# Eight small stores for the tail of one tile: moving bytes between DMA engines in a store-bound attention-score kernel

## The chip, the cores and the metric

One core of one Trainium2 chip. The time is device microseconds of one execution; every run told here is in the fast state, except the single run with labels, whose state is unknown. Before: median 204.15 us (204.05 to 204.17) in the first three runs.

## The reference

```python
batch, heads, seq, dim = 8, 8, 512, 64          # q, k: float32
def reference(q, k):
    scale = 1.0 / np.sqrt(q.shape[-1])
    return (np.einsum('bhqd,bhkd->bhqk', q, k) * scale).astype(np.float32)
```

16.8 MB are read and 67.1 MB written, so the stores are four fifths of the traffic.

## The kernel before

The output is made in 32 tiles of 2 MB, eight (`n`) in each of four units (`v`). A tile holds one pair of heads: head `h` on partitions 64h to 64h+63, and on each partition eight rows of 512 scores, 16 KB. Matmuls write two rows of scores (1024 columns) to PSUM, ScalarE and VectorE take turns in scaling them into the tile `o`, and one DMA of 128 rows of 16 KB stores it. Four buffers of `o` rotate.

```python
P = 128; RO = 8; U = S // RO                      # U = 64
out_r = out.rearrange("(v b) (n h) (u i) k -> v (b n) (h u) (i k)", b=2, h=2, i=RO)
out_pool = ctx.enter_context(tc.tile_pool(name="out", bufs=4))
...
def evacuate(dst, src):                           # alternates ScalarE, VectorE
    ...
def scores(v, n):
    kT, qz = ts[v]
    o = out_pool.tile([P, RO, S], f32, name="o")
    for i in range(0, RO, 2):
        ps = psum_pool.tile([P, 2, S], f32, name="ps")
        for w in range(2):
            pinned(nc.tensor.matmul(out=ps[:, w, :], lhsT=qz[:, i + w, n, :],
                                    rhs=kT[:, n].rearrange("d m s j -> d (m s j)"),
                                    start=True, stop=True))
        evacuate(o[:, i:i + 2, :], ps)
        yield
    src = o.rearrange("p i k -> p (i k)")
    nc.sync.dma_start(out=out_r[v, n], in_=src)
```

`qz` holds q of both heads, block-diagonal with zeros, so one matmul over 128 rows makes both heads' scores. Loads, casts and transposes run ahead of this and are not touched.

## Time and profile before

| | before |
|---|---|
| time, us | 204.15 |
| span in the profile, us | 202.3 |
| packets of the data queue q1 | 5760 |
| one 16 KB packet, start to start, us | 0.607 |
| last packet of the last DMA engine, us from the span's start | 201.01 |
| mean of the 16 engines' last packets, us | 198.53 |

The profile lines are in the prediction below. How to read them: in the slices each digit is the busy share of a fortieth of the span; DMA at 9 from end to end with every compute engine lower says that the data movement is the bound. In the groups, the figures before the bar are count and form, after it busy time and mean, and last the idle time before and what ended it. In the table of windows the columns are the window, its length, five engines' busy time, the granted TensorE clock, the mean busy share of the 16 DMA engines and GB/s.

The page says nothing about single DMA engines. The trace has a record of each packet with its start, duration, size and queue, without the engine. In it a packet as a rule starts 3 to 4 ns before another one ends, which is taken for the one ahead of it on its engine, and each transfer of 128 rows gives eight packets and a completion of 4 bytes to each chain; linked so, all records fall into sixteen rows, as many as the page counts DMA engines. "Row" below means such a chain, and where an engine is spoken of, it is such a row. It is worked out from the trace, not printed by it; where two rows end a packet in the same nanoseconds, they could be exchanged.

### The profile page before, as it was taken

The page shows a single profiled execution, that of the slowest core. Times are in us where ns is not written, and L with a number is a line of the kernel's source. Part 1 is how long each engine was busy: PE and PEld are TensorE (multiplying, and loading weights), DVE is VectorE, ACT ScalarE, POOL GpSimd, SP SyncE. Part 2 cuts the span into 40 slices and gives each one's busy share as a digit, 9 for nine tenths or more (in the row PEclk, how much of TensorE's full clock was granted, in tenths as well). Part 3 has the DMA queues.
Part 4 walks back from the last instruction along what each step waited for, and adds up shares of the span by engine and source line. Part 5 has one row for each costly group of instructions (what it writes and reads, how often), then busy time and mean ns, then how long its engine had stood idle before and what let it go on. Part 6 is the DMA issues. An engine that isn't in the chain of part 4 may idle for free.

```text
span 202.3 us, 1549 instructions
## 1 busy us (share of the span) xinstructions
PE 106.1 (52%) x512; PEld 50.2 (25%) x512; DVE 129.6 (64%) x133; ACT 102.5 (51%) x130; POOL 26.8 (13%) x20
## 2 busy tenths in 40 slices
PE   0045557755854755858575575656564677642000
PEld 0034424432211322423222233223121222210000
DVE  6875669987765686878787788777544455553000
ACT  2254457967654448484756666574833344442000
POOL 1037775756000000000000000000000000000000
PEclk9999999978799699797979787896969655695555
DMA  6999999999999999999999999999999999999991
GB/s 214 428 441 428 424 441 421 424 395 434 437 421 434 432 423 431 434 428 428 437 424 431 431 424 434 434 428 431 434 428 428 431 434 428 428 437 429 416 447 75
DMA packets 5768, 83.99 MB, mean 415 GB/s; under 512 B 640, under 2 KB 640, under 8 KB 640
## 3 DMA queue, kind: packets, MB, share of 16 engines
q1 hardware_dynamic: 5760, 83.89, 97.7%
q8 instruction: 4, 0.07, 0.1%
q14 instruction: 4, 0.03, 0.0%
HBM read 16.78 MB, written 67.11 MB: 415 GB/s over the span
## 4 chain that ended last, share of the span: by engine, by line
DMA 52%; ACT 13%; DVE 13%; PE 10%; issue 2%; ACTq 0%; DVEq 0%; SPq 0%
DMA out_dram<-o 52%; ACT o L62 6%; DVE o L64 5%; PE ps L134 5%; ACT qz L99 4%; DVE qz L89 3%; ACT kT L99 3%; PE tp L120 3%; DVE kT L99 3%; PE tp L111 2%; DVE xb L83 1%; DVE qz L99 1%; ACTq L62 0%; DVEq L64 0%; SPq L140 0%
## 5 line engine op out<-in xcount | busy, mean ns | idle before, releaser
L134 PE MATMUL ps<-kT,qz 128*128 128x512 bf16 x256 | 87.3, 470 | 52.4 <-ACT o L62 43.3
L64 DVE TENSOR_SCALAR o<-ps 128x1024 f32<-128x1024 f32 x64 | 78.2, 1225 | 44.1 <-DMA out_dram<-o 28.5
L62 ACT ACTIVATE o<-ps 128x1024 f32<-128x1024 f32 x64 | 63.5, 1022 | 64.3 <-DMA out_dram<-o 50.9
L134 PEld LDWEIGHTS <-qz 128*128 128x128 bf16 x256 | 28.6, 115 | 98.6 <-issue 87.2
L83 POOL CAST xb<-xf 128x2048 bf16<-128x2048 f32 x14 | 26.1, 1893 | 21.5 <-DMA xf<-in_q_dram 18.1
L99 DVE COPY kT<-tp 64x512 bf16<-64x512 bf16 x32 | 22.0, 687 | 4.3 <-PE tp L111 3.8
L99 DVE COPY qz<-tp 64x512 bf16<-64x512 bf16 x32 | 22.0, 687 | 4.2 <-PE tp L120 3.7
L111 PE MATMUL tp<-identity,xb 128*128 128x128 bf16 x128 | 13.0, 267 | 17.0 <-DVE xb L83 11.1
L99 ACT COPY kT<-tp 64x512 bf16<-64x512 bf16 x32 | 18.5, 578 | 5.0 <-PE tp L111 4.7
L99 ACT COPY qz<-tp 64x512 bf16<-64x512 bf16 x32 | 18.5, 577 | 4.2 <-PE tp L120 3.9
L120 PE MATMUL tp<-identity,xb 128*128 128x128 bf16 x128 | 13.3, 271 | 8.1 <-ACT qz L99 4.9
L111 PEld LDWEIGHTS <-xb 128*128 128x128 bf16 x128 | 11.2, 122 | 21.3 <-ACT xb L83 11.1
L120 PEld LDWEIGHTS <-xb 128*128 128x128 bf16 x128 | 11.5, 123 | 12.6 <-issue 9.7
L89 DVE MEMSET qz<- 64x2048 uint32 x4 | 7.1, 1765 | 2.6 <-issue 1.4
L83 ACT CAST xb<-xf 128x2048 bf16<-128x2048 f32 x1 | 1.9, 1898 | 6.7 <-DMA xf<-in_k_dram 6.7
L83 ACT ACT_TABLE_LOAD x1 | 1.3, 1283 | 0.7 <-PEq L181 0.7
L83 DVE CAST xb<-xf 128x2048 bf16<-128x2048 f32 x1 | 1.2, 1227 | 0.0
masks.py:199 POOL TENSOR_SCALAR_AFFINE_SELECT identity<-identity 128x128 bf16<-128x128 bf16 x1 | 0.3, 292 | 0.1
masks.py:197 POOL MEMSET identity<- 128x128 bf16 x1 | 0.2, 205 | 0.3 <-POOLq L181 0.3
L181 POOL MEMSET const-float32-0.0<- 128x1 f32 x1 | 0.1, 98 | 0.2 <-issue 0.2
L181 POOL MEMSET const-bfloat16-1.0<- 128x1 bf16 x1 | 0.1, 101 | 0.0
L181 POOL MEMSET const-uint8-127<- 128x1 uint8 x1 | 0.1, 101 | 0.0
(1 smaller groups left out, 0.1 us busy)
## 6 DMA issues: line engine op xcount, KB each, us to landing
out_dram<-o SPq DMA_DIRECT2D x32, 2048.0 KB, 16.1
xf<-in_k_dram SPq DMA_DIRECT2D x4, 2048.0 KB, 11.3
xf<-in_q_dram SPq DMA_DIRECT2D x4, 2048.0 KB, 12.3
```

The costliest lines, as they stand in the source:

```text
L62: pinned(nc.scalar.mul(out=dst, in_=src, mul=scale))
L64: pinned(nc.vector.tensor_scalar(out=dst, in0=src, scalar1=scale, scalar2=None, op0=mybir.AluOpType.mult))
L83: pinned(copy(out=xb[:, :, s, :], in_=xf[:, s].rearrange("p (j d) -> p j d", j=J)))
L89: nc.vector.memset(qz[half(h), :, :, (1 - h) * U:(2 - h) * U], 0.0)
L99: pinned(copy(out=dst(s, h), in_=src[:, h]))
L111: pinned(nc.tensor.transpose(out=tp[:, j, :], identity=identity, in_=kb[:, j0 + j].rearrange("p s d -> p (s d)")))
L120: pinned(nc.tensor.transpose(out=tp[:, i, jj, :], identity=identity, in_=qb[:, RO * jj + i0 + i].rearrange("p s d -> p (s d)")))
L134: pinned(nc.tensor.matmul(out=ps[:, w, :], lhsT=qz[:, i + w, n, :], rhs=kT[:, n].rearrange("d m s j -> d (m s j)"), start=True, stop=True))
L181: nc = _bacc.Bacc("TRN2", target_bir_lowering=False, num_devices=1)
```

## The change

Its intent: the sixteen DMA engines don't end together, and a full 128-partition store gives each the same bytes (eight 16 KB packets a row in the trace). So one store (tile 14) leaves out the last 3 KB of each partition. These scores are computed in another place instead, on partitions 0 to 63 for both heads, and stored by eight DMAs of eight partitions, each issued beside a later tile.

```diff
+    out_u = out.rearrange("(v b) (n h) (u i) k -> v (b n) u h (i k)", b=2, h=2, i=RO)
+    LOW = 768
+    low_at = (1, 6)
+    T_LOW = low_at[0] * N + low_at[1]                       # tile 14
+    low = low_pool.tile([U, 2, LOW], f32, name="low")
...
+    def low_scores(v, n, low):
+        for h in range(2):
+            ps = psum_pool.tile([P, 2, S], f32, name="ps")
+            for w in range(2):
+                c0 = (1 - w) * (2 * S - LOW)
+                pinned(nc.tensor.matmul(out=ps[:U, w, c0:], lhsT=qz[half(h), RO - 2 + w, n, h * U:(h + 1) * U],
+                                        rhs=keys[half(h), c0:], start=True, stop=True,
+                                        tile_position=(h * D, 0)))
+            evacuate(low[:, h, :], ps[:U].rearrange("u w k -> u (w k)")[:, 2 * S - LOW:])
+            yield
+    def store_low(v, n, low, r, s):
+        u = slice(32 * r + s, 32 * (r + 1), 4)              # eight partitions, 4 apart
+        nc.sync.dma_start(out=out_u[v, n, u, :, RO * S - LOW:], in_=low[u])
...
+            if (v, n) == low_at and i == RO - 2:            # last step of tile 14: 256 columns, then low
+                ...
+                yield from low_scores(v, n, low)
+                break
...
+        if t == T_LOW:
+            nc.sync.dma_start(out=out_r[v, n, :, :RO * S - LOW], in_=src[:, :RO * S - LOW])
+            return
         nc.sync.dma_start(out=out_r[v, n], in_=src)
+        if T_LOW < t <= T_LOW + 8:
+            store_low(*low_at, low, (t - T_LOW - 1) // 4, (t - T_LOW - 1) % 4)
```

More of the change, by code (lines that the diff above doesn't have):

```diff
@@ L49 @@
     out_pool = ctx.enter_context(tc.tile_pool(name="out", bufs=4))
+    low_pool = ctx.enter_context(tc.tile_pool(name="low", bufs=1))
     tpsum_pool = ctx.enter_context(tc.tile_pool(name="tpsum", bufs=2, space=bass.MemoryType.PSUM))
@@ L125, in transpose @@
                                  .rearrange("d i n (m s jj) -> d s i n m jj", s=2, jj=JJ)[:, s])
+    def low_scores(v, n, low):
+        kT, qz = ts[v]
+        keys = kT[:, n].rearrange("d m s j -> d (m s j)")
+        for h in range(2):
[10 more added lines that the diff above has]
+        nc.sync.dma_start(out=out_u[v, n, u, :, RO * S - LOW:], in_=low[u])
     def scores(v, n):
@@ L130, in scores @@
         o = out_pool.tile([P, RO, S], f32, name="o")
+        keys = kT[:, n].rearrange("d m s j -> d (m s j)")
         for i in range(0, RO, 2):
+            if (v, n) == low_at and i == RO - 2:
+                c1 = 2 * S - LOW
+                ps = psum_pool.tile([P, 2, S], f32, name="ps")
+                pinned(nc.tensor.matmul(out=ps[:, 0, :c1], lhsT=qz[:, i, n, :], rhs=keys[:, :c1],
+                                        start=True, stop=True))
+                evacuate(o[:, i, :c1], ps[:, 0, :c1])
+                yield
+                yield from low_scores(v, n, low)
+                break
             ps = psum_pool.tile([P, 2, S], f32, name="ps")
             for w in range(2):
-                pinned(nc.tensor.matmul(out=ps[:, w, :], lhsT=qz[:, i + w, n, :],
-                                        rhs=kT[:, n].rearrange("d m s j -> d (m s j)"),
+                pinned(nc.tensor.matmul(out=ps[:, w, :], lhsT=qz[:, i + w, n, :], rhs=keys,
                                         start=True, stop=True))
@@ L139, in scores @@
         src = o.rearrange("p i k -> p (i k)")
+        t = v * N + n
+        if t == T_LOW:
+            nc.sync.dma_start(out=out_r[v, n, :, :RO * S - LOW], in_=src[:, :RO * S - LOW])
+            return
         nc.sync.dma_start(out=out_r[v, n], in_=src)
+        if T_LOW < t <= T_LOW + 8:
+            store_low(*low_at, low, (t - T_LOW - 1) // 4, (t - T_LOW - 1) % 4)
     def take(steps, count):
```

## The prediction

> **What bounds the kernel now.** I read four views, in this order: the page's slices and queues, the groups with their idle time, the issues and waits around the stores, and the last microseconds in one-microsecond windows.
>
> The slices and the queue part of the page:
>
> ```profile
> DVE  6875669987765686878787788777544455553000
> ACT  2254457967654448484756666574833344442000
> DMA  6999999999999999999999999999999999999991
> ...
> DMA packets 5768, 83.99 MB, mean 415 GB/s; under 512 B 640, under 2 KB 640, under 8 KB 640
> ...
> q1 hardware_dynamic: 5760, 83.89, 97.7%
> q8 instruction: 4, 0.07, 0.1%
> q14 instruction: 4, 0.03, 0.0%
> ```
>
> DMA is at nine tenths or more from the second slice to the next to last; no compute engine is. The 5760 packets of q1 are 40 transfers of 128 rows of 16 KB (5120 packets) and 640 completion packets, 16 a transfer. Two other queues carry instructions, on the same engines; they matter below.
>
> Groups and waits:
>
> ```profile
> L64 DVE TENSOR_SCALAR o<-ps 128x1024 f32<-128x1024 f32 x64 | 78.2, 1225 | 44.1 <-DMA out_dram<-o 28.5
> L62 ACT ACTIVATE o<-ps 128x1024 f32<-128x1024 f32 x64 | 63.5, 1022 | 64.3 <-DMA out_dram<-o 50.9
> ...
> out_dram<-o SPq DMA_DIRECT2D x32, 2048.0 KB, 16.1
> ```
>
> The evacuations wait for a store to free its buffer (28.5 + 50.9 = 79.4 us), so compute follows the stores. A store lands 16.1 us after its issue, while one store takes the engines about 4.86 us (20 successive landings in the middle are 4.82 to 4.92 us apart): 3.3 stores are queued at any time.
>
> The tail, where the sixteen engines stop being one thing (the last columns are granted clock, DMA share, GB/s):
>
> ```profile
> 195.00:196.00 1.00, 0.00 (x0) 0.00 (x0) 0.00 (x0) 0.00 (x0) 0.00 (x0) 0.50 0.99 426
> 196.00:197.00 1.00, 0.00 (x0) 0.00 (x0) 0.00 (x0) 0.00 (x0) 0.00 (x0) 0.50 0.92 393
> 197.00:198.00 1.00, 0.00 (x0) 0.00 (x0) 0.00 (x0) 0.00 (x0) 0.00 (x0) 0.50 0.84 360
> 198.00:199.00 1.00, 0.00 (x0) 0.00 (x0) 0.00 (x0) 0.00 (x0) 0.00 (x0) 0.50 0.27 115
> 199.00:200.00 1.00, 0.00 (x0) 0.00 (x0) 0.00 (x0) 0.00 (x0) 0.00 (x0) 0.50 0.15 66
> 200.00:201.00 1.00, 0.00 (x0) 0.00 (x0) 0.00 (x0) 0.00 (x0) 0.00 (x0) 0.50 0.04 16
> ```
>
> Compute has ended. From 198 us on a quarter of the engines works, then a seventh, then one. The span is set by the engine that has fallen furthest behind, not by the mean. The trace's packet records give no engine number, but a packet starts 3 to 4 ns before the previous one on its engine ends, so they can be chained into sixteen rows of 320 data and 40 completion packets. Their last completions, in us from the span's start:
>
> ```
> 197.62 197.70 197.74 197.77 197.82 197.83 197.83 198.07 198.09
> 198.64 198.90 199.01 199.06 199.19          200.28          201.01
> ```
>
> The mean is 198.53; the last row ends 2.5 us later. A 16 KB packet takes 0.611 us, starts 0.607 us apart. The chains show why rows fall behind: a 16 KB instruction packet of 0.88 to 1.10 us stands on each of four rows, and data packets next to it are late too (the row ending at 200.28 lost 1.08 us at 32 us, and another 1.8 us in three slow packets up to 42 us). An 8 KB one costs its row 0.30 us and a slowed packet. The last row has one of these late (188.9 us) and some sixty packets that take 0.02 to 0.07 us too long. Seven of the eight latest rows carry instruction packets; of the eight earliest none does.
>
> [...]
>
> **The change part by part.**
>
> *Tile 14's store.* Rows shrink from 16 to 13 KB. Each of the 16 engines is spared 8 x 3072 = 24.6 KB. At 16384 B per 0.607 us, 27.0 KB/us, that is 0.91 us. If 13 KB rows don't keep the rate, it is a little less.
>
> *Eight small stores.* Each reads eight partitions, two runs of 3 KB on each, to 16 runs in HBM. [...] A 3 KB packet at that rate is 0.114 us; with some 5 ns for each packet and each completion (estimate, from 9 ns packets that overlap by 4) a small store costs 2 x 0.119 + 0.005 = 0.243 us, eight cost 1.94 us [...]
>
> *Net.* [...] Bytes in total are the same[...]. Packets: 5120 + 128 data, 640 + 64 completions, 5952 in q1.
>
> *Compute.* Before, the last step of tile 14 is two matmuls of 512 columns and one DVE evacuation (the 60th; even ones are ACT's). Now: one matmul of 256, four with half the rows of 256 + 512 columns for each head, 1792 columns instead of 1024: 768 more at 470/512 = 0.92 ns, +0.7 us of PE[...]. [...] The number of evacuations rises by two, so the alternation after it is as before. ACT waits 50.9/24 = 2.1 us at a time for stores, so this fits into idle time; even a late issue of 1 us meets 3.3 queued stores.
>
> *Issues.* Eight more on SP at 0.33 us. SP waits most of the time for the evacuations, and a small store is issued just behind a large one, its data long ready. Nothing on the path.
>
> *Sum.* What counts is the engine that ends last. If the late rows are the upper engines: 201.01 - 0.91 = 200.10 for the last row; the lower ones (the eight early rows) rise to at most 198.07 + 1.03 = 199.10 and don't take over. Time 204.15 - 0.91 = 203.24 us.
>
> **The rivals.**
>
> (a) *The late rows are the upper engines* (0.65). For it: the layout of the change[...] and the split of eight late and eight early rows, with instruction packets nearly all on the late ones. It gives 203.1 to 203.4.
>
> (b) *The last row is a lower engine* (0.2). The order in which the rows start their first packets is a weak hint for it: one of the rows that may be the last (two of them cross and can't be told apart) starts first of all. Then the end grows by 1.03: 205.2.
>
> (c) *The last is upper, the second a lower engine* (0.1): the row of 200.28 ends at 201.31 instead and the time is 204.45.
>
> (d) *The small stores spread over all 16 engines.* Then nothing is rebalanced and only 64 to 128 completions are added: 204.2. Or the instruction packets shift[...]: plus or minus 0.5 us on one row, on top of any case.
>
> (e) *A compute or semaphore wait takes over*: a small store that waits for an old one, or PE held up by the change of tiling. Against it: 3.3 stores queued; a hole in DMA would need over 13 us of delay.
>
> None of these reaches 2% (4.1 us): even the spread of all rows is 3.4 us.
>
> **Range and chances.** (a) dominates at 203.24; mixed with (b) to (d) the middle is 203.4 us. The low end, 202.9, is (a) with a favourable shift of an instruction packet; the high end, 205.2, takes in (b). Faster by over 2%: 0.01. Within 2%: 0.97. Slower by over 2%: 0.02, for something unforeseen in the small stores.
>
> **What would show it.** The page of the changed kernel should have q1 at 5952 packets, 128 of them between 2 and 8 KB, and the mean evacuation groups split by three new forms. The 3 KB packets mark the lower rows, so the chains then tell which rows are lower: right is (a) if all of the last three are rows without them, and if the tail from 198 us on is about 0.9 us shorter. Rows with 3 KB packets should end about 1 us later than the rest of the early ones did. Evacuations that wait for anything but a store or PE around tiles 14 to 22, or a DMA share under 0.99 between 100 and 160 us, would show (e). I am wrong if the time is over 204.3: then the late engines are lower ones, or the small packets cost more than 0.24 us a store.

As my estimate: I assumed that every small store would lie on the same eight of the sixteen engines, one partition on each, and called these the lower engines, the other eight the upper ones. Eight stores of 0.243 us then put 1.94 us on each lower engine; the shorter rows of tile 14 take 0.91 us off every engine; so a lower one ends 1.03 us later and an upper one 0.91 us earlier. The sum was 204.15 - 0.91 = 203.24 us, and 203.4 with the rivals weighed in. On which rows a store of eight partitions lies, the trace of before doesn't show.

## The result, and the profile after

205.36 us (205.20 to 205.53, 4 runs) against 204.10 of the kernel before on the same chip: slower by 1.26 us, ratio 1.0063 (95% interval 1.0045 to 1.0080). Run again beside later experiments it was 205.27 (205.23 to 205.34). The outputs are correct. The prediction, 203.4 with a range of 202.9 to 205.2, was wrong, and in sign.

First the page of the changed kernel, its slices, packets and issues:

```profile
DMA  6999999999999999999999999999999999999980
...
DMA packets 5960, 83.99 MB, mean 412 GB/s; under 512 B 704, under 2 KB 704, under 8 KB 832
...
q1 hardware_dynamic: 5952, 83.89, 97.0%
...
out_dram<-o SPq DMA_DIRECT2D x1, 1664.0 KB
out_dram<-low SPq DMA_DIRECT2D x8, 48.0 KB
```

5952 packets with 832 - 704 = 128 of 3 KB: the transfers have the form that the prediction worked out. The same bytes, the same full DMA system, and a last slice or two that are emptier than before.

Then the groups, each shape apart, of the evacuations that wait and of the new small work:

```profile
L73 DVE TENSOR_SCALAR o<-ps 128x1024 f32<-128x1024 f32 x63 | 76.9, 1224 | 45.4 <-DMA out_dram<-o 30.1 <-PE ps L172 14.7
L71 ACT ACTIVATE o<-ps 128x1024 f32<-128x1024 f32 x64 | 63.6, 1022 | 65.3 <-DMA out_dram<-o 54.8 <-PE ps L172 9.8 <-PE tp L129 0.2
...
L73 DVE TENSOR_SCALAR low<-ps 64x768 f32<-64x768 f32 x1 | 0.9, 950 | 0.0
L71 ACT ACTIVATE low<-ps 64x768 f32<-64x768 f32 x1 | 0.8, 799 | 0.0
...
L73 DVE TENSOR_SCALAR o<-ps 128x256 f32<-128x256 f32 x1 | 0.4, 425 | 0.0
```

The three odd evacuations took 0.95, 0.80 and 0.42 us, and the large evacuations still wait for stores, now 84.9 us instead of 79.4. Compute is further from the bound, not nearer.

The tail of the changed kernel, in the same windows as before:

```profile
195.00:196.00 1.00, 0.00 (x0) 0.00 (x0) 0.00 (x0) 0.00 (x0) 0.00 (x0) 0.50 1.07 459
196.00:197.00 1.00, 0.00 (x0) 0.00 (x0) 0.00 (x0) 0.00 (x0) 0.00 (x0) 0.50 0.80 344
197.00:198.00 1.00, 0.00 (x0) 0.00 (x0) 0.00 (x0) 0.00 (x0) 0.00 (x0) 0.50 0.61 262
198.00:199.00 1.00, 0.00 (x0) 0.00 (x0) 0.00 (x0) 0.00 (x0) 0.00 (x0) 0.50 0.54 229
199.00:200.00 1.00, 0.00 (x0) 0.00 (x0) 0.00 (x0) 0.00 (x0) 0.00 (x0) 0.50 0.19 82
200.00:201.00 1.00, 0.00 (x0) 0.00 (x0) 0.00 (x0) 0.00 (x0) 0.00 (x0) 0.50 0.04 16
201.00:202.00 1.00, 0.00 (x0) 0.00 (x0) 0.00 (x0) 0.00 (x0) 0.00 (x0) 0.50 0.08 33
```

The emptying starts earlier (0.61 from 197 on, before 0.84) and ends later (an engine still works after 201). The engines have been pulled apart. The 3 KB packets now mark the rows; the last packet of each, in us:

```
rows without 3 KB packets:  196.76 196.82 196.85 197.01 197.05 197.28 198.41 199.44
rows with 16 of them each:  198.73 198.79 198.92 198.99 199.93 200.16 200.17 202.27
```

Ordinary rows without them ended near 197.8 before and end near 197.0 now; ordinary rows with them end at 198.7 to 199.0. That is the predicted motion, down by 0.8 and up by 1.0. But the row that ended last before, the one with many packets a little too long, is among the rows with 3 KB packets: the same pattern now ends at 202.27 instead of 201.01. On it 91 packets of 16 KB took 625 to 690 ns instead of 611, 2.3 us in all; every other row has 6 or fewer. (Before there were 92; 31 of them fell on the row that can't be told apart from it, and the counts depend on where "too long" begins.) The change put load on the slowest row. The row that was second (200.28, with the instruction packet at 32 us) is among the others and went to 199.44.

### The profile page after: what moved, and what is told of

The parts are those of the page before. It is cut to its first block, busy times and chain, and to the rows that moved or that the text cites. A ratio compares the mean times of both kernels' runs of the same rounds, so it can differ in the third digit from the quotient of the medians.

```text
span 203.8 us, 1556 instructions
## 1 busy us (share of the span) xinstructions
PE 104.7 (51%) x506; PEld 50.2 (25%) x515; DVE 129.7 (64%) x134; ACT 103.4 (51%) x131; POOL 26.8 (13%) x20
## 3 DMA queue, kind: packets, MB, share of 16 engines
q1 hardware_dynamic: 5952, 83.89, 97.0%
## 4 chain that ended last, share of the span: by engine, by line
DMA 55%; ACT 16%; PE 9%; DVE 8%; issue 3%; ACTq 0%; SPq 0%
DMA out_dram<-o 55%; ACT o L71 7%; ACT qz L108 5%; ACT kT L108 4%; PE ps L172 4%; DVE qz L98 3%; PE tp L129 3%; DVE o L73 2%; PE tp L120 2%; DVE kT L108 1%; DVE xb L92 1%; ACTq L71 0%; SPq L181 0%
## 5 line engine op out<-in xcount | busy, mean ns | idle before, releaser
L172 PE MATMUL ps<-kT,qz 128*128 128x512 bf16 x245 | 83.6, 465 | 53.2 <-ACT o L71 44.4
L73 DVE TENSOR_SCALAR o<-ps 128x1024 f32<-128x1024 f32 x64 | 77.3, 1212 | 45.4 <-DMA out_dram<-o 30.1
L172 PEld LDWEIGHTS <-qz 128*128 128x128 bf16 x254 | 28.1, 114 | 97.4 <-issue 86.9
L144 PE MATMUL ps<-kT,qz 64*64 64x256 bf16 (+1 forms) x4 | 1.3, 422 | 0.0
L73 DVE TENSOR_SCALAR low<-ps 64x768 f32<-64x768 f32 x1 | 0.9, 950 | 0.0
L71 ACT ACTIVATE low<-ps 64x768 f32<-64x768 f32 x1 | 0.8, 799 | 0.0
```

What stands on the lines that cost most here:

```text
L71: pinned(nc.scalar.mul(out=dst, in_=src, mul=scale))
L73: pinned(nc.vector.tensor_scalar(out=dst, in0=src, scalar1=scale, scalar2=None, op0=mybir.AluOpType.mult))
L144: pinned(nc.tensor.matmul(out=ps[:U, w, c0:], lhsT=qz[half(h), RO - 2 + w, n, h * U:(h + 1) * U], rhs=keys[half(h), c0:], start=True, stop ...
```

## The experiments

My theory: the small stores lie on the same eight rows whatever partitions they read, the row with the slow packets is one of these, and the end is that row's bytes. Rivals: the small stores or the odd compute are dear in themselves; or the row is picked by partition. Each timed run stands beside five rounds of the kernel before. The expectations: their lower or lowest engines are, as in the prediction, the rows that I assumed would take the small stores.

**Which row is which.** The small loads label the rows: sixteen distinct counts tell sixteen rows apart.

```diff
# on the kernel before
+        if 9 <= t < 24:
+            c = 24 - t
+            nc.sync.dma_start(out=marks[:c, c % 5, :256], in_=q_m[:c, :256])
+        if t == 24:
+            nc.sync.dma_start(out=marks[64:67, 0, :320], in_=q_m[:3, :320])
```

> The kernel before, plus one tiny load beside each store of tiles 9 to 23, of 15, 14, ... 1 partitions with 1 KB each, and at tile 24 one of three partitions at 64 to 66 with 1.25 KB. Nothing but labels for the engines. If the number of rows alone picks the engines[...], then sixteen chained rows of packets carry 0, 1, 2, ... 15 of the 1 KB packets[...], and the 1.25 KB packets lie on the three rows with the most. [...] Theory 'one slow lower engine': the row that ends last, with tens of packets 0.02 to 0.07 us too long, has 8 or more of the small packets[...]. Time within 0.5 us of before (204.1).

204.73 us in one run, a little over the 0.5 us that I allowed. Queues of this kernel:

```profile
DMA packets 6014, 84.11 MB, mean 414 GB/s; under 512 B 763, under 2 KB 886, under 8 KB 886
...
q1 hardware_dynamic: 6006, 84.02, 97.6%
```

886 - 763 = 123 labels: 15 + 14 + ... + 1 = 120 and three. The rows carry 0 to 15 of the 1 KB ones, each count once, and the 1.25 KB packets from partitions 64 to 66 lie on the three rows with 15, 14 and 13. Read as one packet of a load on a row, as the three of 1.25 KB lie, the counts say that a load of c partitions lay on the c rows with the most labels. So in this run the number of partitions decided which rows a load used, and in the one load that tried it (partitions 64 to 66) their place did not. The trace has no engine numbers. The expectations below call the row with m labels engine 15 - m; that is a name for a row of this run, no more. The last packets in us:

```
labels  15     14     13     12     11     10     9      8
        198.28 198.75 198.25 199.60 201.66 199.54 200.00 197.96
labels  7      6      5      4      3      2      1      0
        198.01 198.00 198.09 198.00 197.99 200.66 199.30 198.29
```

The row with the slow packets (96 of 625 to 690 ns; no other row has more than one) has 11 labels ("engine 4" below). The late rows do not make a half at all: those with 12, 11, 10 and 9 labels are among the eight with most labels, those with 2 and 1 are not.

**Without the small stores** (wrong; the bytes stay unwritten).

```diff
-        if T_LOW < t <= T_LOW + 8:
-            store_low(*low_at, low, (t - T_LOW - 1) // 4, (t - T_LOW - 1) % 4)
```

> The changed kernel without its eight small stores: the last 3 KB of each row of one tile stay unwritten, wrong on purpose; the extra matmuls and evacuations stay. Theory 'bytes on the last engine': every row ends 0.91 us earlier than before, 203.2 us, 2.1 below the changed kernel. Rival 'the tiling change of PE and the three evacuations hold something up': the time stays within 0.3 us of the changed kernel's 205.4, or at least over 204.1.

203.49 us (203.34 to 203.58), ratio 0.9969 (0.9957 to 0.9982): 0.55 below before, 1.87 below the changed kernel. With all of the odd compute in place it is faster than before, so the compute holds nothing up. Its tail:

```profile
198.00:199.00 1.00, 0.00 (x0) 0.00 (x0) 0.00 (x0) 0.00 (x0) 0.00 (x0) 0.50 0.12 49
199.00:200.00 1.00, 0.00 (x0) 0.00 (x0) 0.00 (x0) 0.00 (x0) 0.00 (x0) 0.50 0.12 49
200.00:201.00 1.00, 0.00 (x0) 0.00 (x0) 0.00 (x0) 0.00 (x0) 0.00 (x0) 0.50 0.00 0
```

After 200 us almost nothing moves: the slow row ends at 200.29, 0.72 before that of the kernel before. I had expected 0.91 in the time and got 0.55; part of what is missing, the closing part of the span, comes up again below.

**The small stores without the saving.**

```diff
                 yield from low_scores(v, n, low)
-                break
...
-            nc.sync.dma_start(out=out_r[v, n, :, :RO * S - LOW], in_=src[:, :RO * S - LOW])
+            nc.sync.dma_start(out=out_r[v, n], in_=src)
```

> The changed kernel with tile 14 also computed and stored whole, so the 3 KB are stored twice with the same values: only what was added, nothing removed. Theory 'bytes on the last engine': the lowest eight rows get 1.94 to 2.1 us more than before, the upper ones nothing, 206.0 to 206.3 us, some 0.9 over the changed kernel. Rival 'small stores are costly in themselves, by waits': the step from no small stores to eight is well over 2.1 us.

206.05 us (206.01 to 206.23), ratio 1.0096 (1.0080 to 1.0111): 2.01 over before, as bytes on the last engine ask for (1.94 to 2.1). The slow row, 16 small packets on it, ended at 203.06. One part missed: the ordinary rows without small packets ended near 198.5, 0.7 later than before, not unchanged. They are not on the path and I have no cause for it. Nor is this run a clean addition. Tile 14's store and the small ones now write the same bytes, and the first small store waited for that store; the waits of SP say so (us in all, times, longest):

```profile
SPq L153 <- DMA out_dram<-o: 9.6, 1, 9.6
```

SP issued nothing from 108.4 to 118.0 us, and the stores came late and close together after it. The DMA engines stayed full (share 1.01 from 108 to 125 us), so the wait opened no hole; whether it has to do with the 0.7 is not shown.

**The same stores from the other half.** The 3 KB are computed on partitions 64 to 127.

```diff
-                pinned(nc.tensor.matmul(out=ps[:U, w, c0:], ... tile_position=(h * D, 0)))
-            evacuate(low[:, h, :], ps[:U] ...)
+                pinned(nc.tensor.matmul(out=ps[U:, w, c0:], ... tile_position=(h * D, U)))
+            evacuate(low[U:, h, :], ps[U:] ...)
...
-        nc.sync.dma_start(..., in_=low[u])
+        nc.sync.dma_start(..., in_=low[U:][u])
```

> The changed kernel with the 3 KB computed on partitions 64 to 127 and stored from there by eight stores of eight partitions, 4 apart, as before. If the number of rows picks the lowest engines, the small packets lie on the same eight rows as in the changed kernel, the slow one among them, and the time is 205.4 (205.1 to 205.7). If the partition picks the engine, they lie on the upper engines, the slow lower one is relieved by 0.91, and the end is 203.2 or where an upper row ends (200.28 + 1.03 = 201.3 from the start of the span, 204.4 us).

205.31 us (205.22 to 205.33), ratio 1.0059 (1.0046 to 1.0071). The slow row carries 16 of the 3 KB packets again and ends at 202.02. So moving the data to the upper partitions did not take the load off the slow row. It did something else. The stretch in which the small stores run, first in the changed kernel (its second profile), then in this one:

```profile
120.00:160.00 40.00, 22.07 (x98) 9.38 (x98) 26.75 (x27) 22.45 (x28) 0.00 (x0) 0.86 1.01 430
```

```profile
120.00:160.00 40.00, 23.12 (x93) 9.76 (x94) 25.82 (x27) 22.45 (x28) 0.00 (x0) 0.81 1.01 416
```

DMA is as busy in both, but moves 14 GB/s less here. Between 105 and 165 us 64 packets of 16 KB took 0.68 to 1.01 us instead of 0.61, against three in the changed kernel; as far as the chains can tell they are on the rows without small packets, next to the small stores, and these rows end at 199.95 to 201.37 instead of 196.8 to 199.4. The cause is not shown; the busy share doesn't tell.

**Half the dose.** 1.5 KB instead of 3 KB, still eight stores.

```diff
-    LOW = 768
+    LOW = 384            # with the last step cut at column 640 instead of 256
```

> The changed kernel with 1.5 KB instead of 3 KB left out of the rows (LOW 384), everything else alike. Theory 'bytes on slow engine 4': lower engines -0.455 + 8 x (2 x 0.062 + 0.005) = +0.58 us instead of +1.03, so 204.6 (204.4 to 204.85), half of what the change cost. Rival 'a fixed cost of having eight more stores': the loss stays at 1.1 to 1.3 us, 205.2 or more.

204.93 us (204.77 to 205.11), ratio 1.0041 (1.0027 to 1.0055). The loss is 0.89 instead of the changed kernel's 1.23 beside it: less, but more than the half that I expected (204.4 to 204.85), and less than the whole loss that the rival foresaw. In the profile the slow row ends at 201.51; 201.01 before and 202.08 in the changed kernel. On that row it is half (0.50 us of 1.07). In this execution (204.77 us, the lowest of the five) and in that of the changed kernel the time between the last packet and the end of the span is 0.18 us longer than before; some 0.2 us of the median is left without a shown cause.

**Giving the bytes to four other rows.** A version that should beat both: 1.5 KB left out, computed in groups of sixteen rows onto partitions 0 to 15, and stored by eight DMAs of four partitions. In the run with labels, read as above, the load of four lay on the rows with 12 to 15 labels, and the slow row has 11; if these stores lie so too, it is relieved.

```diff
-    LOW = 768
+    LOW = 384
...
+            for a0 in range(0, 4, 2):
+                for w in range(2):
+                    c = h * U + 16 * (a0 + w)
+                    pinned(nc.tensor.matmul(out=ps[:16, w, :LOW], lhsT=qz[half(h), RO - 1, n, c:c + 16], ...))
+                evacuate(low[:, h, a0:a0 + 2, :], ps[:16, :, :LOW])
...
-        nc.sync.dma_start(out=out_u[v, n, u, :, RO * S - LOW:], in_=low[u])
+        dst = out_u[v, n].rearrange("(a i s) h x -> s h i a x", a=4, s=4)
+        nc.sync.dma_start(out=dst[s][h, :, :, RO * S - LOW:], in_=low[s:16:4, h])
```

> 1.5 KB left out of the rows, but computed onto partitions 0 to 15 (four groups of rows a head) and given back by eight stores of four partitions, 4 apart. If such a store takes engines 0 to 3 alone, these get -0.455 + 8 x (4 x 0.062 + 0.005) = +1.57 us, all others, the slow engine 4 with them, -0.455. In the run with marks engines 0 to 3 ended at 198.3, 198.8, 198.3, 199.6 and engine 4 at 201.7 us: end 0.45 us earlier than before, 203.6 (203.4 to 203.85). Rows with the small packets: four, the slow one not among them. If the slow engine were one of 0 to 3[...], 204.5 to 206.

203.72 us (203.68 to 203.86), correct, ratio 0.9981 (0.9969 to 0.9994): faster than before by 0.32, than the changed kernel by 1.55. Packets of this kernel, and its tail:

```profile
DMA packets 5929, 84.00 MB, mean 416 GB/s; under 512 B 672, under 2 KB 800, under 8 KB 800
```

```profile
199.00:200.00 1.00, 0.00 (x0) 0.00 (x0) 0.00 (x0) 0.00 (x0) 0.00 (x0) 0.50 0.27 115
200.00:201.00 1.00, 0.00 (x0) 0.00 (x0) 0.00 (x0) 0.00 (x0) 0.00 (x0) 0.50 0.04 16
201.00:202.00 1.00, 0.00 (x0) 0.00 (x0) 0.00 (x0) 0.00 (x0) 0.00 (x0) 0.50 0.00 0
```

800 - 672 = 128 small packets lie on four rows, 32 each, which end at 199.23, 199.78, 200.31 and 200.45. The slow row (78 slow packets) has none and ends at 200.79: still last, but 0.22 earlier than before (0.45 was expected) and 1.3 to 1.5 earlier than in the changed kernel. The same means, aimed at other rows and with half the bytes, turns the sign; the half dose on eight engines had lost 0.89. It is a gain of a fifth of a per cent, all the same.

**Small stores from GpSimd.** An attempt to spare the slow row 0.91 us with four-partition stores, but issued from GpSimd. On which rows these would lie I assumed; no run shows it; both expectations, and the times in them, rest on it.

```diff
+            nc.gpsimd.dma_start(out=dst[s][h, :, :, RO * S - LOW:], in_=low[h * U + s:h * U + 16:4])
+            nc.gpsimd.dma_start(out=tiny[:, 2 * s + h, :], in_=q_t[:4])
```

> 3 KB left out of the rows as in the change, computed onto partitions 0 to 15 (first head) and 64 to 79 (second), given back by eight stores of four partitions issued from GpSimd; after each of them a tiny load of four partitions, also from GpSimd. [...] Then the end is 0.8 to 0.9 us before that of the kernel before, 203.2 (203.0 to 203.5). [...] Rival: [...]sharing of two queues costs more than is gained: over 204.

204.63 us (204.58 to 204.91), ratio 1.0029 (1.0016 to 1.0041). A failed run: the tiny loads, which depend on nothing, had been moved to the start of the program, so the order that I wanted did not exist. Again, with the order kept:

```diff
-            nc.gpsimd.dma_start(...)
+            pinned(nc.gpsimd.dma_start(...))     # both
```

> The run with GpSimd's stores again, with stores and tiny loads kept in program order; in the first try the tiny loads had been moved to 5 to 14 us[...]. [...]the last packet ends 0.5 to 0.9 us before that of the kernel before, 203.2 to 203.6 us. Rival: the bookkeeping packets of GpSimd's queue (544 of them in the first try, 0.4 us later than the even split would give) eat most of it: 203.8 or more.

204.81 us (204.70 to 204.93), ratio 1.0033 (1.0020 to 1.0045). The rival fits better: q0, the queue of GpSimd's DMAs, has 640 packets here, 544 of them under 512 B. But they could not be put on rows with certainty, so it stays open whether the stores landed elsewhere than meant or these packets ate the gain.

**The fixed rest.** In the traces the time from the last packet to the end of the span has two values. It is 1.28 to 1.37 us, or 1.48 to 1.49, and then ScalarE's drain in the closing barrier lasts 127 to 142 ns instead of 14 and starts some 0.28 us later. All five traces with the long one (the changed kernel twice, without small stores, mirror, half dose) had 193 ScalarE records, and no other had. (The limits in the expectations below are a little loose.) So I made 193 out of the kernel before and 195 out of the changed one, with copies of one column at the start.

```diff
     make_identity(nc, identity)
+    pad = consts.tile([P, 1], f32, name="pad")           # 2 in the changed kernel
+    for j in range(1):
+        pinned(nc.scalar.copy(out=pad[:, j:j + 1], in_=identity[:, j:j + 1]))
```

> The kernel before with one ScalarE copy of a 128x1 column more, at the very start where ScalarE waits for its data; nothing of the change. In the traces so far all five kernels with 193 ScalarE records (the changed one, without small stores, mirror, half) have a drain of ScalarE of 127 to 142 ns in the closing barrier and end 1.48 to 1.53 us after the last packet; those with 191, 192, 195 and 197 have a drain of 14 ns and end 1.24 to 1.36 us after it. Theory 'an extra 0.2 us comes from where ScalarE's instructions end': with 193 records the closing part is 1.48 to 1.53 us and the time 204.04 + 0.2 = 204.2 to 204.3. Rival 'the 0.2 us comes with the extra stores or evacuations': time 204.0 to 204.1, drain 14 ns. If it has 194 records, this decides nothing.

> The changed kernel with two such copies more: 195 ScalarE records. Theory of the closing barrier: drain 14 ns, closing part 1.24 to 1.36 us, 205.27 - 0.2 = 205.05 (204.95 to 205.15). Rival: still 205.2 to 205.35.

The traces follow: with 193 records the kernel before has the drain of 128 ns and closes 1.49 us after its last packet; with 195 the changed one has 14 ns and 1.28 us. The times don't decide it. The kernel before with one copy more took 204.25 us (204.19 to 204.31) against 204.10, ratio 1.0005 (0.9991 to 1.0018); the changed kernel with two more 205.24 (205.05 to 205.34), ratio 1.0051 (1.0038 to 1.0064) against the earlier 1.0057. 0.2 us is within what the slow row itself varies by. So the closing part is shown in the profile and not in the time, and why the number of records should matter is not shown.

## Why the prediction was wrong

- **The step that failed** is rival (a), "The late rows are the upper engines", given 0.65. Its two grounds were the layout of the change and the split into eight late and eight early rows. The second was a coincidence: in the run with labels the late rows have 12, 11, 10, 9, 2 and 1 labels. The case that came true is (b), "The last row is a lower engine", given 0.2: the last row carries 16 packets of 3 KB and ends at 202.27 instead of 201.01. For (b) there was a hint in the order of first packets; that hint would have been worth nothing either, since in the run with labels the first to start was not the slow row.
- **What decided it could have been measured before.** Nothing in the profile of before names a DMA engine. The prediction said so, and then chose; a run with labels would have told.
- **The removal, 0.91 us from every row**: 13 KB packets take 0.498 us instead of 0.611, eight of them 0.90 us less. Right. The run without the small stores shows 0.72 on the slow row and 0.55 in the time, and in the profile the closing part (1.49 us instead of 1.31) makes up the rest.
- **The addition, 1.94 us on the eight rows with small stores**: a 3 KB packet took 0.121 us, and the next one started 0.118 us after it. From the run without small stores to the changed kernel the time rises by 1.87, and alone, on top of the kernel before, they add 2.01. Right.
- **Which rows take the small stores**: right in that they are eight (rows with 16 packets of 3 KB each in the changed kernel). That the half of the partitions didn't matter is shown for three partitions by the labels (64 to 66 on the rows with 15, 14 and 13), and for eight by the stores from the upper partitions, 16 packets of which lay on the slow row again.
- **The net of (b), +1.03 us**: the slow row rose by 1.26 in the first profile and 1.07 in the second. On top comes the closing part, 1.31 us before and 1.49 after, which no step had. 1.07 + 0.18 = 1.25 fits the 1.23 to 1.26 measured, but the sum is of one profile: with the closing part back at 1.28 the changed kernel still took 205.24. Either way it lies just over the upper end of the range, 205.2.
- **Compute hidden**: right. The **issue** of a small store was taken as 0.33 us and takes 1.24 to 1.34 us on SP; it was mis-sized fourfold and hidden all the same, as SP waits for evacuations. In the changed kernel (shortest, median, longest in ns):

```profile
L153 SPq DMA_DIRECT2D out_dram<-low x8: 1257/1282/1337, 107.2 to 141.5; - x8
```

- **Rivals (d) and (e)**: no spread over 16 rows, no hole in DMA (share 1.01 from 120 to 160 us in the second profile). That fits case (e)'s argument that the queued stores cover a hold-up: SP's wait of 9.6 us in the run without the saving left no hole either.

What stays open: why some eighty to a hundred of the slow row's packets are 0.01 to 0.07 us too long in a run. A row of this kind ended last in every trace in which the rows could be chained to the end, always one of those with small packets where stores of eight partitions tell it. That it is the same row each time is not shown, as no trace numbers the engines: 11 labels it had in one run, and in the version with stores of four partitions it was not among the four rows with small packets, which fits. It fits also that in every such trace, with labels or without, the last row is the one that carries a single 8 KB instruction packet (q14 on the page of before: 4 packets, 0.03 MB), late (154 to 189 us).

## What to carry to other kernels

Here sixteen rows were full and one ended last, and the time followed that row's bytes: 0.89 to 2.01 us more with small stores on it, 0.32 us less with them on four others. Find out which it is, with a few tiny labelled transfers of 1 to 15 partitions, before shifting load. A load of c partitions, c from 1 to 15, here lay on the c rows with the most labels (as the 120 labels were read above), and the one from partitions 64 to 66 on the three with 15, 14 and 13, which makes a handle for spreading load, and a trap. What can be had this way is small: the gap from the mean row to the last was 2.5 us of 204, and the version that aimed well got 0.3 of it.
